# A third output tile begun before attention ends, in banks of turned tiles, with the seventh mixed row loaded first and eight low parts made on GpSimd

## The chip, the cores and the metric

The kernel runs on one core of a Trainium2 chip. The metric is the device time of one execution in microseconds (us). The profile uses short names for the engines: PE (TensorE), DVE (VectorE), ACT (ScalarE), POOL (GpSimd) and SP (SyncE, whose queue issues nearly all DMAs here). Each engine works through its own instructions in the order of the program and waits at an instruction whose inputs or whose place are not ready.

## The reference

One decoder layer over 1024 positions of 1024 features, in float32. Two groups of eight heads (a banded one with sinks, and a causal one with forget gates) give one mixed value of 1024 features; then come the output projection and a feed-forward part:

```
mixed = jnp.concatenate([out_a.reshape(b, s, A_Q_W), out_b.reshape(b, s, B_W)], axis=-1)
x = x + jnp.einsum('bse,ed->bsd', mixed, w_out)          # h
hn = rmsnorm(x, mlp_norm_g)
hid = jnp.square(jax.nn.relu(jnp.einsum('bsd,df->bsf', hn, w_up)))
x = x + jnp.einsum('bsf,fd->bsd', hid, w_down)
```

## The kernel before

**Number format.** Every float32 matrix product is made of three: each operand is split into a high part (a rounded copy, mostly cast on ACT) and a low part (the operand less its high part, on DVE or POOL), and high·high, high·low and low·high are summed in PSUM. `split` (L77 the cast, L80 the subtraction) does this; `mm` (L73) is every matmul.

**Stages.** The input projection; attention group A; attention group B in units of `scores_b` and `mix_b` (turned score tiles `tpb`, products `pvb`); the output projection (`po`); the up products (`pu`), where seven products of half matrices, in the order 1, 2, 3, 6, 7, 5, 4, take the place of eight; and the down products (`pd`).

**The output projection.** The mixed value lies turned (features on partitions) as eight rows e = 0..7 of 128 features, each a tile [high, low] of 1024 positions (`mix0` to `mix7`). Row 7 is made in SBUF; the others go through DRAM (`mixs_d`) and come back by `load_mix(e)` into named places: m1, m2, m3 for e = 4, 5, 6. The output has eight tiles dt of 128 features by 1024 positions, two PSUM banks each (`po0`, `po1`). For each dt, `out_first` does e = 0..3 beside the attention units and leaves the sum in DRAM (`part_d`). The rest, e = 4..7, is 24 matmuls of 128x512 per tile: for dt 0 and 4 they are begun before the last units of group B end (the list `ahead_of`, in banks of their own), and dt 1, 5, 2, 6, 3, 7 follow in a loop. `out_weights` loads and splits the weights; the i-th goes to place w1 or w0 in turn.

**After each output tile** comes `out_finish(dt, ps)`: `h` is loaded from `part_d`, DVE adds both banks to it (L940 before), `h` is stored to `h_d`, and then the operands `bh[n]`, `bl[n]` (n = 1..7) of the up products are made: `h_split` for n = 1, 2, 3 (DVE low parts, L930), sums `ts` (L947, L959) and `sum_splits` for n = 5, 6, 7, 4 (casts on ACT, low parts on DVE). `bl5` and `bl4` are such low parts. Tiles dt and dt+4 form a pair; the sums need both.

**PSUM.** Eight banks. During attention `pa` holds three banks of turned tiles (tag tr), two of scores (tag sc) and one for `pvb`; `pm0` has the last two. When attention closes, all eight become the pool `pm`, whose tiles `bank(...)` go round. A new tile in a bank waits until the earlier tile's readers are done.

**What sets the order.** A scheduler orders each engine's instructions from modelled times, held by `tc.issue_after(mark)` and priorities; SP's DMAs are in one queue. `up_load(j)` loads the raw up weights (`wur`) to place r0 or r1 in turn, the first one after dt 2's `h` load.

Of the kernel before, what the change touches and what calls it, by code (L numbers as in the profile page):

```python
# [8 lines left out]
F32 = mybir.dt.float32  # L9
F32R = mybir.dt.float32r  # L10
# [6 lines left out]
P = 128  # L17
D = 1024
S = 1024
KT = D // P  # L20
# [35 lines left out]
def hybrid_layer(  # L56
# [13 lines left out]
    nc = tc.nc  # L70

    def mm(out, lhsT, rhs, start, stop):
        return nc.tensor.matmul(out, lhsT, rhs, start=start, stop=stop)  # L73

    def split(hi, lo, src, hi_eng, lo_eng):
        if hi_eng is nc.scalar:
            hi_eng.copy(hi, src)  # L77
        else:
            hi_eng.tensor_copy(hi, src)
        lo_eng.tensor_tensor(out=lo, in0=src, in1=hi.bitcast(F32), op=ALU.subtract)  # L80
# [77 lines left out]
    def w_tiles(n):  # L158


        w = wp.tile([P, 2 * WL], F32R, tag="w", name="w", bufs=8)
        wr = wp.tile([P, WN], F32, tag="wr", name="wr", bufs=3)
        lo = 384 if n == 384 else 400
        return wr[:, :n], w[:, :n], w[:, lo : lo + n]
# [10 lines left out]
    for k in range(KT):  # L175
        xr = ap2.tile([P, S], F32, tag="s", name="xr", bufs=NS)
        wr, wh, wl = w_tiles(384)
# [32 lines left out]
    pa = psa.enter_context(tc.tile_pool(name="pa", bufs=1, space=PSUM, reuse_waits="tile"))  # L210
# [96 lines left out]
    marks = []  # L307
# [263 lines left out]
    def split_mix(e):  # L571


        got = {}

        def load():
            for c in range(2):
                cs = slice(c * 512, (c + 1) * 512)
                m, q = got[c] = [
                    ap2.tile([P, 512], dt, tag=n, name=n, bufs=2)  # L580
                    for n, dt in (("mixr", F32), ("mixn", F32R))
                ]
                nc.sync.dma_start(m, mix_d[e][:, cs])
                for h in range(2):
                    nc.sync.dma_start(
                        q[rows_of[h], :].bitcast(F32), rd_d[2 * e + h, cs].partition_broadcast(HD)
                    )

        def make(c):
            m, q = got[c]  # L590
            lo = ap2.tile([P, 512], F32R, tag="mixs", name="mixs", bufs=1)
            with tc.issue_after(mixed[-1]):
                nc.vector.tensor_tensor(out=m, in0=m, in1=q.bitcast(F32), op=ALU.mult)
            split(q, lo, m, nc.scalar, nc.gpsimd)
            for part_, t in enumerate((q, lo)):
                nc.sync.dma_start(
                    mixs_d[e][part_][:, c * 512 : (c + 1) * 512], t.bitcast(F32)
                )

        return [load, lambda: make(0), lambda: make(1)]  # L600
# [32 lines left out]
    def load_c(p, h):  # L633
        cb = heads[p, "cb", h] = ap2.tile([P, S], F32, tag="bias", name=f"cb{p}{h}", bufs=2)
        nc.sync.dma_start(cb, c_d[2 * p + h].partition_broadcast(P))
# [98 lines left out]
    ended = []  # L734
    mh, ml, mixt = {}, {}, {}
    pend = []

    def prep(f, *a):
        with tc.high_priority(offset=HPA):
            return f(*a)  # L740

    def drain(n):
        while len(pend) > n:
            prep(pend.pop(0))

    def unit(score, mix):
        got = prep(score)
        pend.append(lambda: mix(got))
        drain(DEPTH)
# [3 lines left out]
    def fill(rest=False):  # L753
        while fillers and (rest or fillers[0][0] <= len(marks)):
            fillers.pop(0)[1]()

    def ahead(p, u):
        if p > 3:
            return
        if u == 4:  # L760
            prep(prep_q, p)
        if u == 5:
            prep(prep_k, p, 0)
        if u == 6:
            prep(prep_v, p, 0)
        if u == 7:
            prep(prep_k, p, 1)
# [16 lines left out]
    def heads_b(p):  # L784
        for u in range(8):
            qp, h = (ORDER_END if p == 3 and u > 3 else ORDER_B)[u % 4], u // 4
            unit(lambda: scores_b(p, qp, h), lambda got, qp=qp, h=h: mix_b(got, p, qp, h))
            if u == 1:
                load_c(p, 1)
            if u == DEPTH:  # L790
                prep(prep_v, p, 1)
                if p:
                    prep(inverse_to, 6 + 2 * p, dn_b[(p - 1) % 2], 2)
                else:
                    prep(inverse_a)
            for step in [st.pop(0) for st in splitting if st]:
                step()
            if (p, u) in SPLITS:
                splitting.append(split_mix(SPLITS.index((p, u))))
                splitting[-1].pop(0)()  # L800
            ahead(p + 1, u)
            fill()

# [6 lines left out]
    def slot(tag, name, shape, dt=F32, pool="zl"):  # L810
        return o[pool].tile([P] + shape, dt, tag=tag, name=name, bufs=1)
# [11 lines left out]
        for e in range(4):  # L823
            load_mix(e)

    MIX = {7: "m0", 0: "m1", 1: "m2", 2: "m3", 3: "m4", 4: "m1", 5: "m2", 6: "m3"}

    def mix_tiles(e):
        m = mixt[e] = slot(MIX[e], f"mix{e}", [2, S], F32R)
        mh[e], ml[e] = m[:, 0, :], m[:, 1, :]  # L830

    def load_mix(e):
        mix_tiles(e)
        nc.sync.dma_start(mixt[e].bitcast(F32), mixs_d[e].rearrange("c p s -> p c s"))
# [3 lines left out]
    def out_weights(dt, e0):  # L838
        i = nout[0] = nout[0] + 1
        wr = o["zl"].tile([P, 4, P], F32, tag="wor", name="wor", bufs=2)  # L840
        nc.sync.dma_start(wr, w_o[dt][:, e0 : e0 + 4, :])
        w = slot(f"w{i % 2}", "wos", [2, 4, P], F32R)
        split(w[:, 0], w[:, 1], wr, nc.scalar, nc.gpsimd)
        return w[:, 0], w[:, 1]

    def out_products(ps, w, es):
        wh, wl = w
        for e in es:
            j = e % 4
            for c in range(2):  # L850
                cs = slice(c * 512, (c + 1) * 512)
                mm(ps[c], wh[:, j, :], mh[e][:, cs], j == 0, False)
                mm(ps[c], wh[:, j, :], ml[e][:, cs], False, False)
            for c in range(2):
                cs = slice(c * 512, (c + 1) * 512)
                mm(ps[c], wl[:, j, :], mh[e][:, cs], False, j == 3)

    def first_banks():
        return [o["pm0"].tile([P, 512], F32, tag=f"m{c}", name=f"po{c}") for c in range(2)]

    def out_first(dt):
        xt = slot(f"w{2 + dt % 2}", "xt", [S])
        nc.sync.dma_start(xt, xT[dt * P : (dt + 1) * P, :])
        w = out_weights(dt, 0)
        ps = first_banks()
        with paced():
            out_products(ps, w, range(4))
        t = slot("w4", "pc", [S])
        for c in range(2):
            cs = slice(c * 512, (c + 1) * 512)  # L870
            nc.scalar.copy(t[:, cs], ps[c])
            nc.gpsimd.tensor_tensor(out=xt[:, cs], in0=xt[:, cs], in1=t[:, cs], op=ALU.add)
        nc.sync.dma_start(part_d[dt], xt)
# [9 lines left out]
    for p in range(4):  # L883
        heads_b(p)
    fill(True)
    load_mix(6)

    ahead_of = []
    for dt in (0, 4):
        ps = first_banks() if dt == 0 else [  # L890
            pa.tile([P, 512], F32, tag="sc", name=f"po{c}", bufs=2) for c in range(2)
        ]
        ahead_of.append((dt, ps, out_weights(dt, 4)))

    def beside(n, mark, *es):
        _, ps, w = ahead_of[n]
        with tc.issue_after(mark):
            out_products(ps, w, es)

    beside(0, marks[-1], 4, 5)  # L900
    beside(0, ended[-1], 6)
    beside(1, ended[-1], 4)
    drain(1)
    beside(1, ended[-1], 5)
    drain(0)
    beside(1, ended[-1], 6)
    for dt, ps, w in ahead_of:
        out_products(ps, w, [7])

# [9 lines left out]
    bh, bl = {}, {}  # L919
# [46 lines left out]

    def sum_splits(ts, t, which):
        for i, n in which:
            split(bh[n][:, t], bl[n][:, t], ts[:, i], nc.scalar, nc.vector)

    for dt, ps, w in ahead_of:
        out_finish(dt, ps)
# [4 lines left out]
    raws, up_loads = {}, {}  # L977

    def up_load(j):
        raws[j] = slot(f"r{j % 2}", "wur", [2, KT, P])  # L980
        for i in range(2):
            up_loads[j] = nc.sync.dma_start(raws[j][:, i], w_u[j + i * NJ])

    for dt in (1, 5, 2, 6, 3, 7):
        w = out_weights(dt, 4)
        ps = [bank(f"po{c}") for c in range(2)]
        out_products(ps, w, range(4, 8))
        out_finish(dt, ps)
        if dt in (2, 3):
            with tc.issue_after(part["load"].ins):  # L990
                up_load(dt - 2)
# [20 lines left out]
    def up(j):  # L1012
        if 0 < j < NJ - 1:
            up_load(j + 1)
# [243 lines left out]
    for i in range(len(STEPS)):  # L1258
        down(i)
        if STEPS[i][0] == len(PHASES) - 1 and late:  # L1260
            name, dt, cs = late.pop(0)
# [63 lines left out]
```

## Time and profile before

| | us |
|---|---|
| three runs | 1098.94, 1099.37, 1097.46 (median 1098.94) |
| the profiled execution | 1097.17, of which the span is 1095.5 |
| PE busy in the span | 1081.4 (99%) |
| DVE busy | 774.7 (71%) |
| ACT busy | 571.6 (52%) |
| POOL busy | 365.2 (33%) |

How to read it: the page gives busy time per engine over one profiled execution. In a timeline row the first number is the start, the second the length, then engine, line of the kernel, operation, out<-in, shape and count; a bracket tells the idle time ahead of the row and what ended it. In a table of windows each row is a stretch, then its length, then the busy time of PE, PE's weight loads, DVE, ACT and POOL (with counts), the granted TensorE clock, and the DMA share with GB/s.

### The profile page before, as it was taken

To read this page: it belongs to the slowest core of one execution; us is meant where nothing else is said; L and a number is where in the kernel's file an instruction comes from. 1 tells how busy PE (TensorE), PEld (TensorE's weight loads), DVE (VectorE), ACT (ScalarE), POOL (GpSimd) and SP (SyncE) were. 2 spreads that over 40 slices of the span, in tenths; PEclk is the share of its full clock that TensorE was granted. 3 is DMA by queue.
4 is the path that set the end of the run, shared out by engine and by line. 5 is a ranking of instruction groups with operands and counts; after the bars stand their busy time and mean duration, and the time that the engine had idled before them with its cause. 6 is when DMAs were issued, how large, how long until landed. Compare 5 with 4: busy or idle time off the path is not lost.

```text
span 1095.5 us, 15678 instructions
## 1 busy us (share of the span) xinstructions
PE 1081.4 (99%) x5557; PEld 934.0 (85%) x5557; DVE 774.7 (71%) x1327; ACT 571.6 (52%) x1013; POOL 365.2 (33%) x352
## 2 busy tenths in 40 slices
PE   9999999999998999999999999999999999999998
PEld 8999999999996888778888888888888888888886
DVE  8377677766777883898686869765665867674395
ACT  5558588676767764554545454443633433333331
POOL 5672523435433564223223232332222222222100
PEclk9999999999999999999999999999999999999999
DMA  8401212334347457663554443344898876665423
GB/s 301 146 23 52 71 38 61 115 93 149 116 154 279 156 174 280 228 214 127 195 194 177 172 165 143 144 173 144 311 391 312 306 288 230 233 224 186 174 91 115
DMA packets 96079, 195.69 MB, mean 179 GB/s; under 512 B 7376, under 2 KB 19584, under 8 KB 96000
## 3 DMA queue, kind: packets, MB, share of 16 engines
q1 hardware_dynamic: 95856, 194.66, 50.9%
q8 instruction: 44, 0.72, 0.3%
q14 instruction: 35, 0.29, 0.1%
q10 hardware_dynamic: 144, 0.02, 0.0%
HBM read 141.61 MB, written 53.04 MB: 178 GB/s over the span
## 4 chain that ended last, share of the span: by engine, by line
PE 86%; DVE 6%; DMA 5%; issue 1%; ACT 1%; POOL 1%; SPq 0%; ACTq 0%; DVEq 0%
PE pd L73 27%; PE pu L73 27%; PE ps L73 13%; PE po L73 5%; PE spb L73 3%; PE pvb L73 3%; PE tpb L705 3%; DMA xr<-in_xT_dram 1%; PE sp L73 1%; PE pv L73 1%; DMA xq<-in_x_dram 1%; PE tpa L534 1%; DMA h_d<-h 1%; PE ptk L302 1%; DVE bl L80 1%
## 5 line engine op out<-in xcount | busy, mean ns | idle before, releaser
L73 PE MATMUL pd<-hx,wx 128*128 128x512 f32 (+1 forms) x1350 | 304.9, 388 | 0.0
L73 PEld LDWEIGHTS pd<-hx,wx 128*128 128x128 f32 x1350 | 252.7, 188 | 52.2
L73 PE MATMUL pu<-bh,wu 128*128 128x512 f32 x896 | 276.5, 390 | 1.1 <-ACT wu L77 1.1
L73 PEld LDWEIGHTS pu<-bh,wu 128*128 128x128 f32 x896 | 168.2, 188 | 36.6 <-ACT wu L77 1.6
L73 PE MATMUL ps<-w,xh 128*128 128x384 f32 (+1 forms) x640 | 176.0, 345 | 0.7 <-DVE z L431 0.6
L73 PE MATMUL pu<-bl,wu 128*128 128x512 f32 x448 | 174.5, 390 | 0.6 <-DVE bl L80 0.6
L77 ACT CAST hx<-hr 128x1024 fp32r<-128x1024 f32 x56 | 58.9, 1052 | 176.6 <-PE pd L73 170.6
L80 POOL TENSOR_TENSOR wx<-wda,wx 128x1024 fp32r<-128x1024 f32 x24 | 64.5, 2686 | 196.4 <-ACT wx L77 169.1
L80 DVE TENSOR_TENSOR hx<-hr,hx 128x1024 fp32r<-128x1024 f32 x56 | 72.3, 1299 | 72.4 <-ACT hx L77 72.4
L73 PEld LDWEIGHTS ps<-w,xh 128*128 128x128 f32 x640 | 115.3, 189 | 3.1 <-DVE z L431 1.0
L73 PE MATMUL ps<-w,xl 128*128 128x384 f32 (+1 forms) x320 | 109.8, 344 | 0.0
L73 PEld LDWEIGHTS pu<-bl,wu 128*128 128x128 f32 x448 | 84.1, 188 | 19.2 <-DVE bl L80 1.0
L73 PE MATMUL po<-mix,wos 128*128 128x512 f32 x384 | 94.0, 395 | 1.0 <-ACT wos L77 0.7
L80 POOL TENSOR_TENSOR wu<-wus,wu 128x512 fp32r<-128x512 f32 x32 | 47.2, 1476 | 127.2 <-ACT wu L77 127.2
L73 PEld LDWEIGHTS po<-mix,wos 128*128 128x128 f32 x384 | 70.4, 188 | 15.5 <-ACT wos L77 1.1
L80 POOL TENSOR_TENSOR wu<-wur,wu 128x512 fp32r<-128x512 f32 x32 | 43.3, 1354 | 88.7 <-ACT wu L77 88.7
L77 ACT CAST wu<-wus 128x512 fp32r<-128x512 f32 x64 | 38.4, 618 | 58.8 <-PE pu L73 55.1
L374 DVE TENSOR_TENSOR ptl<-tpb,pth 128x512 fp32r<-128x512 f32 (+1 forms) x80 | 49.3, 631 | 25.1 <-ACT pth L373 23.1
L999 DVE TENSOR_TENSOR ht<-hb 128x512 f32<-128x512 f32 x32 | 21.8, 722 | 63.2 <-ACT hb L1054 63.2
L80 POOL TENSOR_TENSOR w<-wr,w 128x384 fp32r<-128x384 f32 (+1 forms) x47 | 51.5, 1106 | 41.2 <-ACT w L77 29.3
L77 ACT CAST wx<-wda 128x1024 fp32r<-128x1024 f32 x56 | 58.2, 1044 | 6.7 <-DMA wda<-in_w_d_dram 6.6
L73 PEld LDWEIGHTS ps<-w,xl 128*128 128x128 f32 x320 | 60.3, 188 | 1.0
(214 smaller groups left out, 1935.9 us busy)
## 6 DMA issues: line engine op xcount, KB each, us to landing
wda<-in_w_d_dram SPq DMA_DIRECT2D x34, 1024.0 KB, 9.0
hr<-hid_d SPq DMA_DIRECT2D x56, 512.0 KB, 6.0
wur<-in_w_u_dram SPq DMA_DIRECT2D x32, 512.0 KB, 4.3
hid_d<-ht SPq DMA_DIRECT2D x16, 1024.0 KB, 4.3
hid_d<-hb SPq DMA_DIRECT2D x16, 768.0 KB, 3.6
mix<-mixs_d SPq DMA_DIRECT2D x7, 1024.0 KB, 7.4
wr<-in_w_b_dram SPq DMA_DIRECT2D x32, 192.0 KB, 2.5
xr<-in_xT_dram SPq DMA_DIRECT2D x16, 256.0 KB, 4.8
```

What stands on the lines that cost most here:

```text
L73: return nc.tensor.matmul(out, lhsT, rhs, start=start, stop=stop)
L77: hi_eng.copy(hi, src)
L80: lo_eng.tensor_tensor(out=lo, in0=src, in1=hi.bitcast(F32), op=ALU.subtract)
L302: nc.tensor.transpose(pt[:w, j * P : (j + 1) * P], x[:, 4 * c + j, col : col + w], ident)
L374: nc.vector.tensor_tensor(out=lo[:, cols], in0=pt[:, cols], in1=hi[:, cols].bitcast(F32), op=ALU.subtract)
L534: nc.tensor.transpose(tp[:, hh * P : (hh + 1) * P], pts[hh // 2][:, hh % 2, c0 : c0 + P], ident)
L705: nc.tensor.transpose(tp[:, c0 : c0 + P], probs[qi][:, kb * P : (kb + 1) * P], ident)
L999: eng.tensor_tensor(out=out, in0=a, in1=b, op=ALU.subtract)
```

## The change

Three edits. **Row 6 first:** `load_mix(6)` is issued after unit 6 of the last head pair, ahead of the loads of rows 4 and 5, to place r0 and not m3; so the first `up_load` goes to m3. **A third tile ahead:** dt 1 leaves the loop and is begun beside dt 0 and dt 4, in two of the three tr banks, with its weights in w6 (and dt 5's in w5); all tiles now take their rows in the order 6, 4, 5, 7. **GpSimd:** the low parts of operands 5 and 4, two for each of the four pairs of tiles, go from DVE to POOL.

```diff
+            if (p, u) == (3, 6):
+                load_mix(6)
...
-    MIX = {7: "m0", 0: "m1", 1: "m2", 2: "m3", 3: "m4", 4: "m1", 5: "m2", 6: "m3"}
+    MIX = {7: "m0", 0: "m1", 1: "m2", 2: "m3", 3: "m4", 4: "m1", 5: "m2", 6: "r0"}
...
-        w = slot(f"w{i % 2}", "wos", [2, 4, P], F32R)
+        w = slot(f"w{i % 2 + (5 if i in (11, 12) else 0)}", "wos", [2, 4, P], F32R)
...
-                mm(ps[c], wh[:, j, :], mh[e][:, cs], j == 0, False)
+                mm(ps[c], wh[:, j, :], mh[e][:, cs], e in FIRST_OUT, False)
...
+    FIRST_OUT = (0, 6)
...
-    load_mix(6)
+
     ahead_of = []
-    for dt in (0, 4):
-        ps = first_banks() if dt == 0 else [
-            pa.tile([P, 512], F32, tag="sc", name=f"po{c}", bufs=2) for c in range(2)
-        ]
+
+    def begin(dt, ps):
         ahead_of.append((dt, ps, out_weights(dt, 4)))
+
+    def pa_banks(tag, n):
+        return [pa.tile([P, 512], F32, tag=tag, name=f"po{c}", bufs=n) for c in range(2)]
+
+    begin(0, first_banks())
+    begin(4, pa_banks("sc", 2))
...
-    beside(0, marks[-1], 4, 5)
-    beside(0, ended[-1], 6)
+    beside(0, marks[-1], 6)
+    beside(1, marks[-1], 6)
+    beside(0, ended[-1], 4)
+    drain(1)
+    beside(0, ended[-1], 5)
     beside(1, ended[-1], 4)
-    drain(1)
+    drain(0)
     beside(1, ended[-1], 5)
-    drain(0)
-    beside(1, ended[-1], 6)
+    begin(1, pa_banks("tr", 3))
+    beside(2, ended[-1], 6, 4, 5)
     for dt, ps, w in ahead_of:
         out_products(ps, w, [7])
...
-            split(bh[n][:, t], bl[n][:, t], ts[:, i], nc.scalar, nc.vector)
+            split(
+                bh[n][:, t], bl[n][:, t], ts[:, i], nc.scalar,
+                nc.gpsimd if n in (5, 4) else nc.vector,
+            )
...
-        raws[j] = slot(f"r{j % 2}", "wur", [2, KT, P])
+        raws[j] = slot(f"r{j % 2}" if j else "m3", "wur", [2, KT, P])
...
-    for dt in (1, 5, 2, 6, 3, 7):
+    for dt in (5, 2, 6, 3, 7):
         w = out_weights(dt, 4)
         ps = [bank(f"po{c}") for c in range(2)]
-        out_products(ps, w, range(4, 8))
+        out_products(ps, w, (6, 4, 5, 7))
```

**PE, where the third tile ends and the loop's first tile begins, with the waits each row carries.** In the changed program the tiles `po_5704` and `po_5705` are dt 1's two banks, `po_5820` and `po_5821` dt 5's; `mix_4258` is row 7, `mix_5500` row 6.

```order
L73 MATMUL po_5704<-mix_4258,wos 128x512 x2
L73 MATMUL po_5705<-mix_4258,wos 128x512 x2
L73 MATMUL po_5704<-mix_4258,wos 128x512
L73 MATMUL po_5705<-mix_4258,wos 128x512
L73 MATMUL po_5820<-mix_5500,wos 128x512 [waits DVE_49]
L73 MATMUL po_5820<-mix_5500,wos 128x512
```

In the kernel before, dt 1 (`po_5778`, `po_5779`) and dt 5 (`po_5820`, `po_5821`) begin so, `mix_5442` being row 4:

```order
L73 MATMUL po_5778<-mix_5442,wos 128x512 [waits Activation_49]
L73 MATMUL po_5778<-mix_5442,wos 128x512
L73 MATMUL po_5779<-mix_5442,wos 128x512 [waits DVE_49]
L73 MATMUL po_5779<-mix_5442,wos 128x512
L73 MATMUL po_5820<-mix_5442,wos 128x512 [waits Activation_49]
L73 MATMUL po_5820<-mix_5442,wos 128x512
L73 MATMUL po_5821<-mix_5442,wos 128x512 [waits PE_49]
L73 MATMUL po_5821<-mix_5442,wos 128x512
```

Before, dt 5's first product waits for a cast of its weights. After the change its first bank is the tr bank that holds dt 1's right half (`po_5705`), and the product waits for a count of finished DVE instructions: the one that reaches it is the add that reads `po_5705`.

**DVE, from the first add to h on.** Before, with dt 0's two adds, dt 4's first one and dt 0's `bl1` ahead of these rows (`h_5737` is dt 0's h, `h_5748` dt 4's, `h_5804` dt 1's; the number after `po` tells the half, that after `bl` the operand):

```order
L940 TENSOR_TENSOR h_5748<-po1_5598,h_5748 128x512
L930 SCALAR_TENSOR_TENSOR bl2_5725<-h_5748,vt_67,bh2_5724 128x512
L947 SCALAR_TENSOR_TENSOR ts_5744<-h_5737,vt_67,b12_5745 128x512
L959 SCALAR_TENSOR_TENSOR ts_5744<-h_5748,vt_67,b12_5745 128x512
L930 SCALAR_TENSOR_TENSOR bl3_5727<-h_5748,vt_67,bh3_5726 128x512
L959 SCALAR_TENSOR_TENSOR ts_5744<-h_5748,vt_67,ts_5744 128x512
L80 TENSOR_TENSOR bl5_5733<-ts_5744,bh5_5732 128x512
L80 TENSOR_TENSOR bl7_5731<-ts_5744,bh7_5730 128x512
L959 SCALAR_TENSOR_TENSOR ts_5744<-h_5748,vt_67,ts_5744 128x512
L80 TENSOR_TENSOR bl6_5729<-ts_5744,bh6_5728 128x512
L80 TENSOR_TENSOR bl4_5735<-ts_5744,bh4_5734 128x512
L940 TENSOR_TENSOR h_5804<-po0_5778,h_5804 128x512
```

After the change (`h_5768` is dt 0's, `h_5779` dt 4's, `h_5799` dt 1's); dt 0's two adds and dt 4's first stand ahead of these rows:

```order
L953 TENSOR_TENSOR h_5779<-po1_5598,h_5779 128x512
L943 SCALAR_TENSOR_TENSOR bl1_5754<-h_5768,vt_67,bh1_5753 128x512
L960 SCALAR_TENSOR_TENSOR ts_5775<-h_5768,vt_67,b12_5776 128x512
L972 SCALAR_TENSOR_TENSOR ts_5775<-h_5779,vt_67,b12_5776 128x512
L943 SCALAR_TENSOR_TENSOR bl2_5756<-h_5779,vt_67,bh2_5755 128x512
L943 SCALAR_TENSOR_TENSOR bl3_5758<-h_5779,vt_67,bh3_5757 128x512
L972 SCALAR_TENSOR_TENSOR ts_5775<-h_5779,vt_67,ts_5775 128x512
L80 TENSOR_TENSOR bl7_5762<-ts_5775,bh7_5761 128x512
L972 SCALAR_TENSOR_TENSOR ts_5775<-h_5779,vt_67,ts_5775 128x512
L80 TENSOR_TENSOR bl6_5760<-ts_5775,bh6_5759 128x512
L953 TENSOR_TENSOR h_5799<-po0_5704,h_5799 128x512
L953 TENSOR_TENSOR h_5799<-po1_5705,h_5799 128x512
```

`bl5` and `bl4` have left DVE's order; dt 1's two adds (the last row is the second) still stand behind all other work on the first pair.

**SP, the loads of rows 4 to 6.** Before, and after the change:

```order
L596 DMA mixs_d_81<-mixs_5397 128x512
L873 DMA part_d_82<-xt_5270 128x1024
L841 DMA wor_5773<-in_w_o_dram 128x512
L834 DMA mix4_5442<-mixs_d_81 128x2x1024
L938 DMA h_5737<-part_d_82 128x1024
L834 DMA mix5_5444<-mixs_d_81 128x2x1024
L834 DMA mix6_5588<-mixs_d_81 128x2x1024
```

```order
L596 DMA mixs_d_81<-mixs_5397 128x512
L879 DMA part_d_82<-xt_5270 128x1024
L836 DMA mix6_5500<-mixs_d_81 128x2x1024
L843 DMA wor_5706<-in_w_o_dram 128x512
L836 DMA mix4_5442<-mixs_d_81 128x2x1024
L951 DMA h_5768<-part_d_82 128x1024
L836 DMA mix5_5444<-mixs_d_81 128x2x1024
```

Row 6 now stands ahead of rows 4 and 5, right behind the last stores of the rows it is made of.

## The prediction

> **What bounds the kernel now.** The page's first part says that PE is busy for 99% of the span. So I looked next at the table of windows over the stretch that the change touches, and over all that follows (columns: start:end, length, then busy time of PE, weight loads, DVE, ACT, POOL, the granted clock, DMA share, GB/s).
>
> ```profile
> span 1095.5 us, 15678 instructions
> PE 1081.4 (99%) x5557; PEld 934.0 (85%) x5557; DVE 774.7 (71%) x1327; ACT 571.6 (52%) x1013; POOL 365.2 (33%) x352
> ...
> 430.00:440.00 10.00, 9.65 (x55) 8.16 (x54) 3.77 (x8) 3.38 (x8) 1.02 (x5) 1.00 0.87 317
> 440.00:450.00 10.00, 9.31 (x42) 7.38 (x41) 8.36 (x11) 5.08 (x9) 3.07 (x2) 1.00 0.50 176
> 450.00:460.00 10.00, 10.00 (x46) 8.28 (x45) 8.99 (x15) 6.17 (x11) 2.59 (x2) 1.00 0.71 238
> 480.00:490.00 10.00, 8.78 (x37) 6.62 (x37) 9.57 (x12) 7.00 (x12) 4.97 (x4) 1.00 0.38 140
> 510.00:786.00 276.00, 276.00 (x1216) 227.83 (x1215) 199.41 (x279) 127.95 (x159) 81.33 (x58) 1.00 0.48 175
> ```
>
> From 510 on PE has no gap. The little to be had lies between 425 and 500, and there DVE works almost without a break as well. PE's waits in 400 to 500 are these five:
>
> ```profile
> PE pu L73 <- ACT wu L77: 1.1, 1, 1.1
> PE po L73 <- ACT wos L77: 0.7, 1, 0.7
> PE pu L73 <- DVE bl L80: 0.6, 1, 0.6
> PE po L73 <- DMA mix<-mixs_d: 0.3, 1, 0.3
> PE pvb L73 <- DVE mtb L722: 0.3, 1, 0.3
> ```
>
> They sum to 3.1 us, visible idle alone. A lost start costs a little more, seen in PE's timeline:
>
> ```profile
> 437.79 5.63 PE L73 MATMUL po<-mix,wos 128*128 128x512 f32 x24
> 444.11 32.93 PE L73 MATMUL po<-mix,wos 128*128 128x512 f32 x144 [0.69 <-ACT wos L77]
> 476.88 0.39 PE L73 MATMUL pu<-bh,wu 128*128 128x512 f32 x1
> 480.96 0.39 PE L73 MATMUL pu<-bh,wu 128*128 128x512 f32 x1
> 482.50 0.50 PE L73 MATMUL pu<-bh,wu 128*128 128x512 f32 x1 [1.15 <-ACT wu L77]
> ```
>
> 144 matmuls from 444.11 to 476.88 are 0.2276 us each, 5.46 per output tile of 24. From 437.79 the 24 matmuls should last to 443.25, so the wait for dt 1's weights cost 0.86; the up wait, 480.96 + 0.23 to 482.50, cost 1.31. In the same way the other three cost 0.58 (mix), 0.53 (mtb) and 0.71 (bl), each its idle time in the list plus a share of one matmul.
>
> **What the change removes.** dt 1's weights now have a place of their own (w6), so the 0.86 goes. The 0.58 is the wait for row 6, in the kernel before the last of three loads:
>
> ```profile
> 419.33 0.33 SPq L596 DMA_DIRECT2D mixs_d<-mixs  x1
> 423.55 0.38 SPq L834 DMA_DIRECT2D mix<-mixs_d  x1
> 425.73 0.92 SPq L834 DMA_DIRECT2D mix<-mixs_d  x2
> mixs_d<-mixs SPq DMA_DIRECT2D x1, 256.0 KB, 2.8
> mix<-mixs_d SPq DMA_DIRECT2D x3, 1024.0 KB, 7.4
> ```
>
> Row 6 can be read from 419.33 + 2.8 = 422.1. Put first in the queue it lands between 4.9 us later, as the first of the three loads did before, and 7.4, their median: 427.0 to 429.5, against 428.2 now. I take the early end, as it is the first in line. Its first product cannot run before the last unit's scores anyway; rows 4 and 5 slip behind it by one load, and their products too stand later. So 0.58 goes, and 0.53 goes with the changed order beside the units, within a bound of 1.0 lost if row 5 is late. Sum 1.97: the three tiles' 72 matmuls, which before ended at 444.11 + 24 x 0.2276 = 449.58, end at 447.6. PE stands ready for dt 5 then.
>
> **What it adds.** The order shown with the change has dt 5's first product wait for a DVE count, and the count is reached by the second add of dt 1's h: dt 5's bank is dt 1's right half. Before, this bank was not dt 1's, and the trace has no such wait. What is queued behind that product on PE is everything: 120 matmuls, then the up stage. So the end of DVE's work ahead of that add decides. These are its rows of before:
>
> ```profile
> 441.42 1.37 DVE L940 TENSOR_TENSOR h<-po,h 128x512 f32<-128x512 f32 x2 [1.66 <-PE po L73]
> 444.88 1.19 DVE L930 SCALAR_TENSOR_TENSOR bl<-h,vt,bh 128x512 fp32r<-128x512 f32 x1
> 445.98 1.77 DVE L947 SCALAR_TENSOR_TENSOR ts<-h,vt,b 128x512 f32<-128x512 f32 x1
> 447.68 0.74 DVE L959 SCALAR_TENSOR_TENSOR ts<-h,vt,b 128x512 f32<-128x512 f32 x1
> 449.67 1.28 DVE L80 TENSOR_TENSOR bl<-ts,bh 128x512 fp32r<-128x512 f32 x2
> 452.91 1.28 DVE L940 TENSOR_TENSOR h<-po,h 128x512 f32<-128x512 f32 x2
> 444.13 3.07 POOL L80 TENSOR_TENSOR wos<-wor,wos 128x512 fp32r<-128x512 f32 x2 [10.04 <-ACT wos L77]
> 467.70 1.42 POOL L80 TENSOR_TENSOR wos<-wor,wos 128x512 fp32r<-128x512 f32 x1 [1.49 <-ACT wos L77]
> 467.89 1.78 DVE L930 SCALAR_TENSOR_TENSOR bl<-h,vt,bh 128x512 fp32r<-128x512 f32 x1
> ```
>
> From the first add, 441.42, to the end of dt 1's second, 454.19, it took 12.77 us. Two low parts (bl5, bl4) leave it, 1.28 for the two by the row at 449.67: 11.5. The first add now starts later than before: dt 1's products of rows 6, 4 and 5 stand ahead of all products of row 7, and row 7's run tile by tile, so dt 0's first bank is done 14 matmuls before PE's end, at 447.6 - 3.2 + 0.2 of latency = 444.6. Then dt 1's bank comes free at 444.6 + 11.5 = **456.1**. Bounds: with no disturbance by POOL the 1.19 and 1.77 would be 0.74, saving 1.5: 454.7. With one POOL instruction more in the way, 1.78 - 0.74 = 1.04 by the last row: 457.1. PE idles 8.5 us (7.1 to 9.5), where before it idled for 0.69.
>
> **The clock.** What such an idle time does is seen at both ends of the trace. PE's last matmul ends in the window at 1090, at about 1090.84, and the granted clock falls 3.4 us later; and the first matmuls of the program start slowly:
>
> ```profile
> 1090.00:1091.00 1.00, 0.84 (x8) 0.63 (x6) 0.96 (x3) 0.00 (x0) 0.00 (x0) 1.00 0.63 236
> 1094.00:1094.20 0.20, 0.00 (x0) 0.00 (x0) 0.00 (x0) 0.00 (x0) 0.00 (x0) 1.00 0.03 5
> 1094.20:1094.30 0.10, 0.00 (x0) 0.00 (x0) 0.00 (x0) 0.00 (x0) 0.00 (x0) 0.57 0.00 0
> 1094.30:1095.00 0.70, 0.00 (x0) 0.00 (x0) 0.00 (x0) 0.00 (x0) 0.00 (x0) 0.50 0.00 0
> 1.28 3.59 PE L73 MATMUL qps<-warm 128*128 128x512 bf16 x8 [1.28 <-DVE warm L171]
> ```
>
> Eight matmuls of 512 columns in 3.59 us are 0.45 each, twice 0.2276. So after 8.5 us of idle PE resumes at half rate, and half of the first 3.6 us is lost: 1.8 (0 if the clock should hold). [...]
>
> dt 5, 2, 6, 3, 7 then take 120 x 0.2276 = 27.3, so the up stage starts at 456.1 + 1.8 + 27.3 = 485.2 against 476.88: **+8.3**.
>
> **The up stage.** Its two waits, 1.31 + 0.71 = 2.0, are for chains that run beside PE from 444 on. With PE 8.3 later these chains have caught up in part. DVE's part: it starts 3.2 late; after 456.1 it has two operations of 0.7 and then nothing until dt 5's products end at 456.1 + 1.8 + 5.5 = 463.4, 5.8 of idle time; but it sheds eight low parts, 8 x 0.64 = 5.1. So it is about 4 late where PE is 8 late, and the wait of 0.71 goes. The ACT wait of 1.31 comes from a cast held by a store:
>
> ```profile
> 473.07 7.55 DMA h_d<-h
> 480.69 0.63 ACT wu L77
> 457.48 5.01 DMA wur<-in_w_u_dram
> ```
>
> That store follows dt 6's adds, which move with PE, so some of the wait stays. In SP's queue `wur` stands behind a load that needs dt 1's h stored; before it was issued 457.48 - 454.19 = 3.3 after dt 1's second add, so now at about 459.4, landing by 464.4, far ahead of 485.2. I leave 1.0 of waits in the up stage (0 to 2.7), so 1.0 is gained.
>
> **GpSimd.** A POOL low part should take the 1.42 us of the POOL row above, off the path: the next product that reads bl5 or bl4 is far behind, in the up stage. Each relieves DVE by 0.64, but the row at 467.89 has a DVE operation from SBUF go from 0.74 to 1.78 beside a POOL one. [...]
>
> **Sum.** -1.97 is inside the 447.6; +8.3 - 1.0 = **+7.3**. Against the profiled execution's own 1097.17 that is 1104.5. The three runs lie 0.29 to 2.20 above the profiled one, on average 1.4 (their median 1.77), so I forecast **1105.9**, and add the same 1.4 to the rivals. Own range, from the bounds 454.7 and 457.1, clock 0 to 1.8 and up waits 0 to 2.7: +3.1 to +10, 1101.7 to 1108.6.
>
> **Rivals.** *No bank wait (faster).* If dt 1's adds were done by 447.6, the gain would be 1.97 and some of the up waits, -2.7 in all: 1095.9. For it: every removed wait is real in the list. Against it: dt 1's products end only at 447.6, so even with dt 1's adds put first they could not be done before 448.9 (1.28 the pair), and here four adds and nine other operations stand ahead. 4%. *A small net change:* the count reached much earlier than the names say, a stall of about 3 us, no clock loss: within 2 us of 1098.9. 4%. *Short stall, clock kept:* DVE undisturbed, bank free at 454.7, no half rate, up waits gone: 454.7 + 27.3 - 476.88 - 2.0 = +3.1: 1101.7. Against it: three and a half idle microseconds sufficed at the end of the trace. 7%. *POOL's low parts stretch DVE:* each of the eight delays a DVE operation by 1.04, 8.3 in all. DVE would be 3.2 + 5.8 - 5.1 + 8.3 = 12.2 late at its end where PE is 8.3 late, so 3.9 of waits in the up stage in place of my 1.0: +10.2, 1108.8. It decides from the point where the delays sum to over 4.4. For it: DVE is 90% busy or more in the windows from 450 on before. Against it: the adds read PSUM, and DVE has idle time while PE makes dt 5. 13%. The forecast keeps 72%.
>
> **The range.** 8 in 10 are held by 1101.4 to 1110.0: the own range, the stretch case with 1 us on top, and a little beyond the short one. A measurement of this kernel can tell 0.2%, 2.2 us. Faster by more 4%, within it 4%, slower 92%.
>
> **What would show it.** In the changed profile: the three early waits gone and 72 `po` matmuls done at 447 to 448; then one gap on PE of 7 to 9.5 us, released by DVE's add to h; a granted clock below 1.00 after it; the up stage starting near 485; and from there a shift that stays to the end. It would be wrong if PE ran on past 448 without that gap, if DVE's add came by 450, or if a new gap, for `bl` or `wu`, of over 3 us stood in the up stage.

## The result and the profile after

The changed kernel takes 1107.05 us (median of 6 runs, 1105.67 to 1110.93) against 1099.41 us for the kernel before (6 runs, 1097.46 to 1102.1): a ratio of 1.0078, 95% interval 1.0063 to 1.0093, or 8.6 us more (6.9 to 10.2). Forecast were 1105.9 us and +7.3. The profiled execution took 1108.79 us, with a span of 1107.1, and that of the kernel before 1097.17. They are 11.6 us apart, 3.0 more than the ratio gives, so a single part below can differ by that much from one execution to the next; the account of the prediction names one that does.

The windows over the stretch that changed (columns as before: start:end, length, busy time of PE, weight loads, DVE, ACT, POOL, granted clock, DMA share, GB/s):

```profile
440.00:450.00 10.00, 10.00 (x51) 8.45 (x50) 2.88 (x6) 3.27 (x7) 2.46 (x2) 1.00 0.27 89
450.00:460.00 10.00, 1.10 (x5) 0.64 (x4) 9.81 (x13) 5.10 (x9) 4.82 (x4) 0.65 0.69 231
460.00:470.00 10.00, 10.00 (x38) 8.06 (x38) 2.61 (x4) 1.57 (x3) 1.28 (x1) 0.83 0.62 213
```

From 450 to 460 PE does 1.1 us of work. DVE, which in the kernel before was busy for 8.36 of the ten microseconds from 440 on, is busy for 2.88 there and full in the next ten; then it has little to do until 470. PE's waits from 400 to 520, and the rows of its timeline that carry them:

```profile
PE po L73 <- DVE h L953: 8.9, 1, 8.9
PE po L73 <- DMA mix<-mixs_d: 2.0, 2, 1.7
PE pu L73 <- POOL wu L80: 1.2, 1, 1.2
PE pu L73 <- ACT bh L942: 0.6, 1, 0.6
...
430.19 2.56 PE L73 MATMUL po<-mix,wos 128*128 128x512 f32 x10 [1.68 <-DMA mix<-mixs_d]
441.09 9.71 PE L73 MATMUL po<-mix,wos 128*128 128x512 f32 x42
459.70 29.19 PE L73 MATMUL po<-mix,wos 128*128 128x512 f32 x120 [8.90 <-DVE h L953]
488.73 0.39 PE L73 MATMUL pu<-bh,wu 128*128 128x512 f32 x1
```

At the 0.2276 us per matmul of the kernel before, the three tiles end at 441.09 + 42 x 0.2276 = 450.65. Then PE waits 8.9 us for DVE's add to h, and the 120 products of the last five tiles take 29.0 us in place of 27.3. The up stage starts at 488.73, where it started at 476.88. On DVE the chain ahead of dt 1's second add:

```profile
447.67 1.29 DVE L953 TENSOR_TENSOR h<-po,h 128x512 f32<-128x512 f32 x2 [4.61 <-PE po L73]
451.12 1.76 DVE L960 SCALAR_TENSOR_TENSOR ts<-h,vt,b 128x512 f32<-128x512 f32 x1
453.46 2.41 DVE L943 SCALAR_TENSOR_TENSOR bl<-h,vt,bh 128x512 fp32r<-128x512 f32 x2
458.36 1.29 DVE L953 TENSOR_TENSOR h<-po,h 128x512 f32<-128x512 f32 x2
466.94 1.29 DVE L953 TENSOR_TENSOR h<-po,h 128x512 f32<-128x512 f32 x2 [5.62 <-PE po L73]
```

Its first add comes at 447.67, after an idle time of 4.61 us in which it waited for PE, and 6.25 us later than in the kernel before. dt 1's adds end at 459.65. Next it is DVE that waits, 5.62 us for dt 5's products. The granted clock, in the windows where it changes:

```profile
452.00:453.00 1.00, 0.00 (x0) 0.00 (x0) 1.00 (x2) 0.03 (x1) 0.33 (x1) 1.00 0.87 324
453.00:454.00 1.00, 0.00 (x0) 0.00 (x0) 1.00 (x2) 1.00 (x2) 0.34 (x1) 0.53 0.97 350
462.00:463.00 1.00, 1.00 (x4) 0.80 (x3) 0.00 (x0) 0.00 (x0) 0.95 (x1) 0.50 0.09 29
463.00:464.00 1.00, 1.00 (x6) 0.77 (x5) 0.00 (x0) 0.00 (x0) 0.33 (x1) 0.85 0.06 20
```

The clock here is 1.00 or 0.50, and a mean between them tells when it changed: 0.53 over the window from 453 puts the fall at 453.06, and 0.85 over that from 463 the return at 463.30.

### The profile page after: what moved, and what is told of

It reads as the page before. It is cut to its first block, busy times and chain, and to the rows that moved or that the text cites. A ratio compares the mean times of both kernels' runs of the same rounds, so it can differ in the third digit from the quotient of the medians.

```text
span 1107.1 us, 15677 instructions
## 1 busy us (share of the span) xinstructions
PE 1083.6 (98%) x5557; PEld 935.4 (84%) x5557; DVE 768.6 (69%) x1319; ACT 572.3 (52%) x1013; POOL 379.3 (34%) x360
## 4 chain that ended last, share of the span: by engine, by line
PE 84%; DVE 6%; DMA 5%; issue 2%; POOL 1%; ACT 1%; SPq 0%; POOLq 0%; DVEq 0%; ACTq 0%
PE pd L73 27%; PE pu L73 27%; PE ps L73 12%; PE po L73 4%; PE spb L73 3%; PE pvb L73 3%; PE tpb L705 2%; DMA xr<-in_xT_dram 1%; PE sp L73 1%; PE pv L73 1%; PE tpa L534 1%; DMA mix<-mixs_d 1%; DMA xq<-in_x_dram 1%; DVE ts L972 1%; PE ptk L302 1%
```

## The experiments

The theory to begin with was the prediction's: PE waits for the bank of dt 1's right half, and pays for the idle time with half the clock. Four runs on the changed kernel tested its parts.

| run | median us | ratio to the kernel before | 95% interval |
|---|---|---|---|
| the changed kernel | 1107.05 | 1.0078 | 1.0063 to 1.0093 |
| e1 other banks | 1105.22 | 1.0044 | 1.0026 to 1.0062 |
| e2 adds first | 1103.55 | 1.0041 | 1.0027 to 1.0054 |
| e3 PE kept busy | 1105.79 | 1.0050 | 1.0035 to 1.0065 |
| e4 low parts on DVE | 1105.46 | 1.0052 | 1.0032 to 1.0071 |
| e5 other banks, low parts on DVE | 1105.50 | 1.0067 | 1.0051 to 1.0082 |
| e6 before, with GpSimd's low parts | 1102.68 | 1.0040 | 1.0025 to 1.0055 |
| e7 before, with row 6 first | 1097.97 | 0.9989 | 0.9979 to 1.0000 |
| e8 row 7 early | 1106.62 | 1.0074 | 1.0059 to 1.0089 |
| e9 third tile behind row 7 | 1101.22 | 1.0020 | 1.0012 to 1.0029 |
| e10 e7 with own weights | 1101.12 | 1.0016 | 1.0005 to 1.0027 |
| e11 e10, `wur` behind the store | 1099.14 | 0.9996 | 0.9987 to 1.0005 |
| e12 e7, `wur` behind the store | 1098.13 | 0.9985 | 0.9973 to 0.9996 |

Runs are compared by their ratios, since each group had its own runs of the kernel before (medians 1098.34 to 1099.76).

### e1: the bank wait taken away

```diff
-    pda.close()
-    psa.close()
-    pm = ctx.enter_context(tc.tile_pool(name="pm", bufs=1, space=PSUM, reuse_waits="tile"))
+    early_banks = {5: first_banks, 2: lambda: pa_banks("sc", 2)}
...
-        ps = [bank(f"po{c}") for c in range(2)]
+        if dt == 6:
+            pda.close()
+            psa.close()
+            pm = ctx.enter_context(
+                tc.tile_pool(name="pm", bufs=1, space=PSUM, reuse_waits="tile")
+            )
+        ps = early_banks[dt]() if dt in early_banks else [bank(f"po{c}") for c in range(2)]
```

> The changed kernel with dt 5 in the two banks that dt 0 had and dt 2 in the two that dt 4 had; dt 1's banks are taken again only by dt 6. Theory (the bank of dt 1's right half is what PE waits for): the gap of 8.9 us ahead of the loop and the half clock after it (1.7 us) go, dt 5 starts within 0.5 us of the end of the three tiles; DVE, which starts its adds some 6 us later than in the kernel before, then gives up to 3 us of waits in the output tiles and the up stage: 1097 to 1101, ratio to the kernel before 0.998 to 1.002. Rival (PE is held by DVE's work whatever the bank, since DVE is full): the gap only moves to dt 6 or to the up stage, 1104 to 1108.

The ratio fell from 1.0078 to 1.0044 only; the time is the rival's. PE's longest waits in 400 to 530, and the windows (columns as above):

```profile
PE po L73 <- POOL wos L80: 2.1, 1, 2.1
PE pu L73 <- DVE bl L943: 1.9, 3, 0.8
PE po L73 <- DVE h L953: 1.2, 1, 1.2
...
450.00:460.00 10.00, 10.00 (x46) 8.29 (x45) 9.72 (x13) 4.74 (x9) 5.01 (x4) 1.00 0.69 239
460.00:470.00 10.00, 8.83 (x40) 6.93 (x39) 9.47 (x13) 5.33 (x9) 3.90 (x4) 1.00 0.76 282
470.00:480.00 10.00, 7.88 (x31) 6.08 (x30) 9.97 (x11) 3.85 (x7) 6.03 (x4) 0.91 0.78 290
490.00:500.00 10.00, 8.26 (x33) 5.54 (x32) 10.00 (x8) 5.69 (x10) 8.62 (x6) 1.00 0.29 102
```

The gap of 8.9 us is gone and PE is full from 450 to 460. So the bank was what PE waited for, as forecast. But the time comes back as seven shorter waits from 460 to 500, 6.4 us in all, while DVE is busy 95 to 100%. That makes DVE, which starts its adds 6 us late, the suspect; e9 puts it to the test. e1 alone does not show it: its longest wait, 2.1 us, is for a low part of weights that POOL makes behind a low part of h, as in e6 below, and a half clock follows it (last section).

### e2: the adds of all three tiles ahead of the splits

```diff
-    for dt, ps, w in ahead_of:
-        out_finish(dt, ps)
+    for dt, h in [(dt, out_add(dt, ps)) for dt, ps, w in ahead_of]:
+        out_split(dt, h)
```

Here `out_finish` is cut in two: `out_add` loads h, adds and stores, `out_split` does the rest.

> The changed kernel with the adds to h of all three tiles called ahead of their splits, dt 1's h in the free place r1; dt 1's second add is then DVE's 9th operation after the last unit and not its 15th. Banks as in the changed kernel. Theory (bank wait, its length set by DVE's place of that add): a gap of about 4 us where the changed kernel has 8.9, about 4.5 to 6.5 us faster in all, with or without the half clock: 1101 to 1103. Rival (the gap comes from dt 1's h, loaded late from DRAM, or from the weights): the gap stays at 8 to 9 us, 1106 to 1108.

```profile
454.51 25.49 PE L73 MATMUL po<-mix,wos 128*128 128x512 f32 x100 [3.99 <-DVE h L954]
```

The gap is 3.99 us, as worked out from DVE's order; so the place of that add sets the gap's length, and neither the load of h nor the weights do. The gain, 0.37% or 4.1 us, is a little less than the 4.5 to 6.5 forecast. The gap is 4.9 us shorter, but the half clock now takes 2.5 us (100 products in 25.3 us, where 22.8 are needed at full rate) in place of 1.7, which leaves 4.1.

### e3: the gap filled with work

```diff
         out_products(ps, w, [7])
+    busy = pa.tile([P, 512], F32, tag="pv", name="busy", bufs=1)
+    for _ in range(36):
+        mm(busy, mh[7][:, :P], mh[7][:, :512], True, True)
```

> The changed kernel with 36 more matmuls of 128x512 (high row 7 by itself, result unused, in the bank of pvb) between dt 1's last product and dt 5's first, to fill 8.2 us of the gap with work. Theory (half clock after the idle time): the granted clock stays at 1.00 through 450 to 470, the 120 matmuls after it take 27.3 us and not 29.0, 1.7 us faster than the changed kernel: 1105 to 1106. Rival (the 29.0 us come from something else, such as weights late in the loop): no change, 1107.

```profile
450.00:460.00 10.00, 9.26 (x42) 7.35 (x40) 9.84 (x13) 5.12 (x10) 5.01 (x4) 1.00 0.72 235
460.00:470.00 10.00, 10.00 (x44) 8.25 (x45) 5.56 (x8) 3.83 (x7) 2.62 (x3) 1.00 0.77 286
459.89 17.56 PE L73 MATMUL po<-mix,wos 128*128 128x512 f32 x76 [0.74 <-DVE h L956]
477.98 10.27 PE L73 MATMUL po<-mix,wos 128*128 128x512 f32 x44 [0.53 <-POOL wos L80]
```

The clock stays at 1.00, and the 76 products behind the gap run at the full 0.23 us each. Over all its runs the mean granted clock is 0.999, where the changed kernel has 0.994. A new wait of 0.53 us for weights ends behind the 76 products, so the loop takes 28.2 us and not 27.3. The ratio fell from 1.0078 to 1.0050, 3.1 us and more than the 1.7 of the clock, but the two intervals just overlap; so the size of the gain is not shown, only what the clock and the profile say.

### e4, e5, e6: the low parts on GpSimd

In e4 (the changed kernel) and e5 (e1) the low parts go back to DVE; e6 is the kernel before with nothing but the move to GpSimd:

```diff
-                nc.gpsimd if n in (5, 4) else nc.vector,
+                nc.vector,
```

> The changed kernel with all low parts of h on DVE again, as before. Theory: the gap changes by less than 1 us (one low part more ahead of dt 1's add, one POOL operation less beside it), and the up stage waits up to 1.5 us more for DVE: 1106 to 1109. Rival (POOL's low parts stretch DVE and are a good part of the loss): 2 to 4 us faster than the changed kernel, 1103 to 1105.

> The kernel of e1 (no wait for dt 1's bank) with all low parts of h on DVE again. In e1 DVE has no idle time from 447.8 to 509, and operations beside POOL's subtractions take about 1.75 us in place of 0.74. Theory (DVE is the bound of this stage since it starts its adds 6 us late, and POOL's eight low parts stretch it by as much as they take off it, 8 x 0.64 = 5.1 us): within 1.5 us of e1, 1103.5 to 1106. Rival (the move does relieve DVE): 4 to 5 us slower than e1, 1109 to 1110.

> The kernel before, with only the eight low parts of operands 5 and 4 moved to GpSimd. Theory (POOL stretches DVE by as much): 0 to 3 us slower than the kernel before, 1099 to 1102. Rival (DVE is relieved by 5.1 us, the wait of 0.7 for a low part in the up stage goes): 0.5 to 1 us faster.

e4: PE's gap in its profile is 8.8 us, as with GpSimd, and the ratio 1.0052 lies between the theory and the rival (interval 1.0032 to 1.0071); the up stage waits 0.2 us in place of 1.8, where the theory had it wait longer.

```profile
456.96 30.05 PE L73 MATMUL po<-mix,wos 128*128 128x512 f32 x120 [8.78 <-DVE h L953]
```

e5 took 1105.50 us, inside its theory's 1103.5 to 1106. By the ratios it stands 2.5 us above e1 (1.0067 against 1.0044), but the two intervals overlap, so whether the move gains anything in that kernel is not shown. In the kernel before (e6) the move alone costs 0.40%, 4.4 us, more than the theory's upper end of 3. PE's waits there that the kernel before does not have, and two rows of POOL:

```profile
PE po L73 <- POOL wos L80: 2.1, 1, 2.1
PE pu L73 <- DVE bl L930: 1.9, 2, 1.1
...
467.11 1.73 POOL L80 TENSOR_TENSOR bl<-ts,bh 128x512 fp32r<-128x512 f32 x1
468.80 1.72 POOL L80 TENSOR_TENSOR wos<-wor,wos 128x512 fp32r<-128x512 f32 x1
```

A low part of h, which nobody needs before the up stage, stands in POOL's queue ahead of a low part of the weights, which PE waits for at 470.5. That I had not priced. Only e6 stands clear of the noise. e4 lies 2.9 us below the changed kernel by the ratios, but their intervals overlap too; so that the move costs something there as well is not shown.

### e7: row 6 first, alone

```diff
+            if (p, u) == (3, 6):
+                load_mix(6)
...
-    MIX = {7: "m0", 0: "m1", 1: "m2", 2: "m3", 3: "m4", 4: "m1", 5: "m2", 6: "m3"}
+    MIX = {7: "m0", 0: "m1", 1: "m2", 2: "m3", 3: "m4", 4: "m1", 5: "m2", 6: "r0"}
...
-        out_products(ps, w, range(4, 8))
+        out_products(ps, w, (6, 4, 5, 7))
```

(with the begun tiles in the order of the change, dt 0 and 4 only, and `wur` in m3.)

> The kernel before, with only row 6 loaded first to r0 and the rows taken in the order 6, 4, 5, 7; no third tile, weights in w1 and w0, low parts on DVE. My prediction took 0.6 to 1.1 us of gain for this part. Theory now (row 6 is the last of the rows to be made, so that taking it first waits for it, 0.5 to 2.0 us by the four profiles with this order): 0 to 1.5 us slower than before, 1099 to 1101. Rival (the prediction): 0.6 to 1.1 us faster.

```profile
PE po L73 <- DMA mix<-mixs_d: 1.7, 1, 1.7
PE po L73 <- ACT wos L77: 0.7, 1, 0.7
...
442.97 1.37 DVE L951 TENSOR_TENSOR h<-po,h 128x512 f32<-128x512 f32 x2 [0.30 <-PE po L73]
```

Ratio 0.9989 (0.9979 to 1.0000). PE does wait 1.7 us for row 6, as the new theory has it, and yet the kernel is not slower. Whether it is a little faster, as the prediction had it, is not shown, since the interval ends at no change. The waits that went are that for `mtb` and half of that for `wu` in the up stage (1.1 before, 0.6 here).

### e8 and e9: where dt 1's products stand

Both are e5 with dt 1's products of rows 6, 4 and 5 called behind those of row 7; in e9 they are also held there:

```diff
-    begin(1, pa_banks("tr", 3))
-    beside(2, ended[-1], 6, 4, 5)
     for dt, ps, w in ahead_of:
         out_products(ps, w, [7])
+    begin(1, pa_banks("tr", 3))
+    with tc.issue_after(last_mm[0].ins):        # e9 only; last_mm: the last product so far
+        out_products(*ahead_of[2][1:], (6, 4, 5, 7))
```

> The kernel of e5 with dt 1's rows 6, 4 and 5 no longer between the last unit and the products of row 7: the scheduler then puts them ahead of the last unit's end and runs row 7 for all three tiles at once. DVE's first add then comes about 4 us earlier after the last unit. Theory (what costs the time is DVE's late start, in a stage where DVE is as full as PE): 3 to 5 us faster than e5 and e1, 1100 to 1102, with under 2 us of waits left in the output tiles. Rival (the loss lies in the rows or the weights): within 1.5 us of e5.

> The kernel of e5 (dt 1 in tr banks with weights in w6, dt 5 and dt 2 in the banks of dt 0 and dt 4, low parts on DVE) with all of dt 1's products held behind the products of row 7 of dt 0 and dt 4. Theory (the loss of e1, e5 and e8 comes from dt 1's 18 products standing ahead of DVE's first add, in a stage in which DVE has no idle time; PE had no idle time there to fill): DVE's first add comes where e7 has it, some 3 us earlier after the last unit than in e5, and the kernel takes 1097 to 1099, 6 to 8 us less than e5, ratio to the kernel before 0.997 to 1.001. Rival (third tile in tr banks, weights in w5 and w6 or the early banks cost by themselves): 1102 or more.

e8 missed. The scheduler moved the 18 products ahead of the last unit, so that unit ended later, and DVE's first add came no earlier:

```profile
447.55 1.37 DVE L953 TENSOR_TENSOR h<-po,h 128x512 f32<-128x512 f32 x2 [0.30 <-PE po L73]
```

That says more than the run was meant to. From PE's first product of row 6 to DVE's first add it is 16.5 us in e8 (431.10 to 447.55) and 17.2 in e5 (428.30 to 445.46), but 12.5 in e7 (430.47 to 442.97). So whether the 18 products stand ahead of the last unit (e8) or behind it (e5), DVE starts 4.0 to 4.7 us later, about their own length: 18 x 0.2276 = 4.1. PE had no idle time in which to do them.

How DVE's lateness gets back to PE is seen at e8's longest wait:

```profile
475.73 0.62 ACT L77 CAST bh<-ts 128x512 fp32r<-128x512 f32 x1 [4.02 <-DVE ts L960]
476.26 0.61 ACT L77 CAST wos<-wor 128x512 fp32r<-128x512 f32 x1
476.92 1.19 PE L73 MATMUL po<-mix,wos 128*128 128x512 f32 x4 [3.89 <-ACT wos L77]
```

PE waits 3.9 us for the cast of the last tile's weights. Their load was issued at 453.8 at the latest and took 5.2 us at most, but the cast stands on ACT behind a cast of `ts`, and that one waits 4.0 us for DVE. In e5 the same two waits are 3.4 us on ACT and 1.9 on PE. In e9 DVE starts as in e7:

```profile
442.26 1.37 DVE L956 TENSOR_TENSOR h<-po,h 128x512 f32<-128x512 f32 x2 [0.30 <-PE po L73]
PE pu L73 <- ACT bh L945: 2.4, 1, 2.4
```

and the ratio falls from 1.0067 (e5) to 1.0020: 5.2 us for nothing but the place of these products. The forecast of 1097 to 1099 was missed by 2 us, which lie in the up stage (the wait of 2.4 us above, for a cast that stands on ACT behind one that waits for a store of h, and behind it a clock of 0.50 from 483.2 to 486.7, with a mean of 0.83 over 480 to 490). So of the 0.67% that e5 loses, the place of these products ahead of DVE's first add is 0.47%.

### e10, e11, e12: is there a version that beats both?

e10 is e7 with the weights' places of the change; e11 and e12 issue the second load of up weights behind the store of dt 6's h, on e10 and on e7:

```diff
-        w = slot(f"w{i % 2}", "wos", [2, 4, P], F32R)
+        w = slot(f"w{i % 2 + (5 if i in (11, 12) else 0)}", "wos", [2, 4, P], F32R)   # e10, e11
...
-            with tc.issue_after(part["load"].ins):
+            with tc.issue_after((part["store", 6] if dt == 3 else part["load"]).ins):   # e11, e12
                 up_load(dt - 2)
```

> The kernel of e7 (row 6 first, nothing else) with dt 1's weights in w6 and dt 5's in w5, so that dt 1 does not wait until dt 0's weights are done with. Theory (the wait of 0.7 us on PE for these weights goes, and POOL's two subtractions at 444 no longer stand beside DVE's first chain, 1.5 us of DVE): 0.7 to 2 us faster than e7, ratio to the kernel before 0.997 to 0.9985. Rival (DVE is the bound and the 0.7 us come back as a wait in the up stage): as e7, 0.9985 to 1.0.

> The kernel of e10 with the second load of up weights issued behind the store of dt 6's h, on which a cast on ACT waits (that store took 7.55 us to land beside this load in the kernel before, and PE waited 1.15 us for the cast). Theory: the store lands in 3 to 4 us, PE's wait for the cast goes, 0.5 to 1.3 us faster than e10. Rival (another chain ends just behind it, DVE's low parts): within 0.3 us of e10.

> The kernel of e7 (row 6 first, nothing else) with the second load of up weights issued behind the store of dt 6's h, as in e11. Theory (in e7 PE waits 0.6 us for a cast that waits for this store; in e11 the same move gained 2 us over e10): the wait goes, 0.5 to 1.5 us faster than e7, ratio to the kernel before 0.9975 to 0.9985. Rival (DVE's low parts are the next to end, 0.8 us in e7): as e7, 0.9985 to 1.0.

e10 missed, on the wrong side of both theories: the wait for dt 1's weights is gone, and the kernel is 0.27% slower than e7. Its waits in the up stage:

```profile
PE pu L73 <- DVE bl L941: 1.7, 2, 1.2
PE pu L73 <- ACT wu L77: 1.4, 1, 1.4
PE pu L73 <- DVE bl L80: 0.6, 1, 0.6
```

These are 3.7 us where e7 had 1.4. A part of the rest is the clock. The first ten products of row 6, in e10 and then in e7:

```profile
429.93 3.91 PE L73 MATMUL po<-mix,wos 128*128 128x512 f32 x10 [1.84 <-DMA mix<-mixs_d]
430.47 2.52 PE L73 MATMUL po<-mix,wos 128*128 128x512 f32 x10 [1.68 <-DMA mix<-mixs_d]
```

In e10's profile the clock is 0.50 from 430.8 to 434.2 (a mean of 0.83 over 430 to 440), behind that wait, which costs 1.4 us and more than takes back the 0.9 gained. Over all runs it is less: the mean granted clock is 0.9981 in e10 and 0.9987 in e7, some 0.7 us of the 3.0 between them. Why the up stage waits 2.3 us longer is not settled. e11 regains 2.2 us (0.9996, its interval just touches e10's), more than its theory asked; e12 stands at 0.9985 (0.9973 to 0.9996), within its theory's range but no clear step from e7's 0.9989. So the best version here is e12, the kernel before with row 6 first and one load moved, 1.6 us (0.15%) faster than the kernel before, which is less than the 0.2% that the prediction took as what can be told.

## Why the prediction was right, and where not

**The bank wait: right.** The gap stands where forecast, released by DVE's add to h, 9.05 us long from 450.65 to 459.70 against 8.5 (7.1 to 9.5). DVE's chain took 11.98 us, forecast 11.5. e1 (other banks) and e2 (adds first) change the gap as the theory says.

**The clock: right in size.** The 120 products took 29.03 us, 1.7 over 27.3, forecast 1.8; e3 shows that it is the idle time: with PE busy for 9.26 of the ten microseconds from 450 on, the clock stays at 1.00. That the slow first matmuls of the program show the same was a reading of mine that no run shows: the granted clock of the kernel before is 1.00 in every window from 0 to 6 us. How the clock falls was wrong (last section).

**The early gain of 1.97: did not come.** The waits of 0.86 and 0.53 are gone, as forecast, though e10 shows that without the first of them alone the kernel is not faster. For the 0.58 two steps failed. The first is a reading: the 0.58 was put down to row 6, the last of the three loads. But in the kernel before dt 0's products begin with row 4, the first load, and that is the one PE waits for. The chain of work of the kernel before has it (start, length, what):

```profile
423.55 4.95 DMA mix<-mixs_d
428.54 1.66 PE po L73 x6
```

Putting row 6 in the first place does not take away a wait for the first load. The second step is "I take the early end", which put row 6's landing at 4.9 us after its issue, as that first load had it. In the changed kernel the issue is at 423.09 and the landing takes 7.0, near the other bound; over the twelve profiles with row 6 first it takes 6.3 to 7.7. PE waited 1.68 us, and the three tiles ended at 450.65, not 447.6. The changed kernel and e1 to e5 run the same program up to there, and in their profiles the tiles end at 448.0 to 450.8, later where row 6 lands later. The kernel before ends the same products at 449.58, and at 450.95 in e6's profile. So no gain is shown, and the scatter of this part is as large as the 3.0 us by which the two profiles differ more than the ratio.

**The up stage: mis-sized.** I left 1.0 us of waits; the changed kernel has 1.8 us of idle time there (0.6 and 1.2), as much as before (1.7). So nothing was gained.

**GpSimd: the wrong place.** I priced DVE operations stretched beside POOL's (0.74 to 1.78 us in one row of the kernel before), and took the move as free otherwise since bl5 and bl4 are needed late. e6 shows that POOL's own queue has something urgent in it. The delays of the stretch rival (13%, 1108.8) are there: in e1's and e6's profiles single DVE operations beside POOL's subtractions take 1.7 to 1.8 us in place of 0.74 (e1 at 451.25 and 463.96, e6 at 447.37 and 450.39). DVE's adds, which read PSUM, keep 0.68 us beside them (e6 at 467.62 and 469.32), as that rival's counter-argument had it. What makes the others slower is not shown, nor, since e4 does not stand clear of the changed kernel, what they cost in it.

**The faster rival: its condition was too weak.** I wrote that without the bank wait the kernel would gain 2.7 us. e1 has no bank wait and is 0.44% slower than the kernel before. The step that failed is the line that DVE "is about 4 late where PE is 8 late": PE is 8 late only because of the gap. Without it DVE's lateness is itself the bound. So of the 0.78% that the change costs, e1 puts 0.34% on the bank wait and its clock, and 0.44% on what is left; e9 against e5 shows 0.47% for the place of dt 1's products. The forecast named the path that the changed kernel takes, but less than half of what the change costs goes away with it; the rest was hidden behind the gap.

**The number: in part luck.** In the profiles the early gain is off by 3.0 us, DVE's chain by 0.5 and the up stage by 1.0, all towards slower, and the two profiled executions are 11.6 us apart where +7.3 was forecast. The medians lie nearer to the forecast because the profile after is of a long execution and that before of a short one.

What stays open: why e10's up stage waits longer than e7's, and what GpSimd's low parts are worth in the changed kernel and in e1.

## What to carry to other kernels

A tile begun ahead is only free if the engine has idle time there. PE's waits ahead of the first result summed to 0.7 us in the kernel before, and 4.1 us of products pulled ahead of that result gave it 4 us later to DVE, which was nearly as full as PE. When a new wait shows, ask what would end last without it before pricing its removal: here a gap of 8.9 us was worth 3.7. And a bank taken over from a tile whose reader stands deep in another engine's queue is a wait on that queue (DVE's, 8.9 us, here), so look up which instruction frees it.

## What the runs showed of the hardware that was not expected

I took 3.4 us of idle time, seen at the end of the kernel before, as what it takes for the clock to fall. In the changed kernel it fell at 453.06, 2.4 us after PE stopped at 450.65, and came back at 463.3, 3.6 us after PE resumed. In e1 it fell behind a wait of 2.12 us, after PE was at work again:

```profile
475.00:475.50 0.50, 0.14 (x1) 0.00 (x0) 0.50 (x1) 0.00 (x0) 0.50 (x2) 1.00 0.87 344
477.00:477.50 0.50, 0.25 (x1) 0.25 (x2) 0.50 (x1) 0.00 (x0) 0.20 (x1) 1.00 0.95 369
478.00:479.00 1.00, 1.00 (x4) 0.76 (x4) 0.97 (x3) 0.00 (x0) 0.00 (x0) 0.57 0.77 279
481.00:482.00 1.00, 1.00 (x5) 0.81 (x4) 1.00 (x3) 0.91 (x3) 0.00 (x0) 0.73 0.96 381
477.25 6.44 PE L73 MATMUL po<-mix,wos 128*128 128x512 f32 x20 [2.12 <-POOL wos L80]
```

PE stops at 475.1 and starts at 477.25; the clock is halved from about 478.1 to 481.5, 3.4 us, and the 20 products take 6.3 us in place of 4.6. The half clock lasts 6.8 us in e2 (453.1 to 460.0) and 10.2 in the changed kernel, two and three times that. What sets when it begins and ends is not shown: it fell 3.4 us after PE stopped at the end of the kernel before, 2.4 us after in the changed kernel, and 3.0 us after in e1, where PE had been back at work for 0.9 us.

A wait of some 2 us was seen to cost 1.7 us more (e1), 1.4 us more (e10) and nothing more (e3). Behind e10's wait of 1.84 us the clock fell, and behind a wait of 2.00 us for the same load in e3 it stayed at 1.00, with a mean of 1.00 over 430 to 440:

```profile
431.00 2.56 PE L73 MATMUL po<-mix,wos 128*128 128x512 f32 x10 [2.00 <-DMA mix<-mixs_d]
```

The clock is also a part of the scatter between executions of one kernel: of the 74 of the kernel before beside e1 to e12, the 33 with a mean granted clock of 0.999 or more have a median of 1097.9 us, and the 14 with 0.997 or less one of 1100.5.
